# A Strassen-type FFN output product: its seven products chained in PSUM, two of them and the context tokens in plain float32

## The chip, the cores and the metric

The kernel runs on one core of a Trainium2 chip. The metric is the device time of one execution in microseconds. A profiled execution has a span, from its first to its last instruction, and granted clocks of TensorE; all rows below come from one such execution of the kernel before.

## What is computed

Two layers of a trunk over 1024 latent tokens and 256 context tokens of width 1024. Each layer mixes tokens (convolution, retention, attention) and ends in a SwiGLU FFN with a norm behind it. The change touches the FFN's second product alone:

```python
def swiglu(h, w1, w2):
    u, gt = jnp.split(h @ w1, 2, axis=-1)
    return (jax.nn.silu(gt) * u) @ w2          # w2: 2816 x 1024

x = x + g2 * rmsnorm(swiglu(latent), post2_g)    # both layers
xc = xc + cg2 * rmsnorm(swiglu(context), post2_g)    # first layer only
```

Everything is float32 in and out.

## The kernel before

A product that has to be exact in float32 is made of three matmuls in a rounded format (`F32R`): an operand x is split by ScalarE into a rounded high part h (`split`, cast at L85) and by VectorE or GpSimd into the rest l = x - h (L80, `tt`), and TensorE adds h*h, l*h and h*l into one PSUM bank (`mms`, L105). A plain `F32` operand can also go into a matmul as it is; the modulation vectors (`mod_mm`, L209) and the attention's weighting (L1037) do that.

The gated values of the FFN lie in DRAM (`gd`, 22 blocks of 128 rows, 1280 tokens in layer 0, 1024 in layer 1). The second product multiplies them with `ffn_out`, 22 row blocks of 128 x 1024. The first 18 blocks (`NB`) go through a seven-product scheme of the Strassen kind on 2 x 2 blocks of 512: tokens in two halves, row blocks in pairs, output columns in two halves. `groups` makes one group of two row blocks (one pair per product) and four of four (two pairs). `operands` loads a group's values A and weights B (`raw`, `gr`, `wr` tiles by SP's DMA queue), makes sums and differences of quarter blocks in place (`each`), splits them (`two`, `both`) into `gh`, `gl`, `wh`, `wl` with four buffers each, and yields the products in the order 1, 2, 7, 6, 5, 3, 4. Three products are prepared ahead of TensorE.

For each product TensorE works through four token tiles, each into its own bank of PSUM (tag `po`: eight banks in the last layer, six in layer 0), and the bank is added into one of 28 accumulators in SBUF (`evacuate`: VectorE, the group 0 a copy by ScalarE at L1525). There is one accumulator set for each of the seven products; after the last group the `fuse` steps, and in the last layer two more steps in the tail, combine them into the four output blocks. Accumulators appear in the trace as `p`.

In layer 0 the 256 context tokens ride along without the scheme: their values (`gc`) are split, and products 1, 0, 2 and 3 of each group each begin with the context's matmuls on the same split weights (tag `cx`, two banks).

The last four row blocks of all tokens are done in the tail, tile by tile, with the norm, the residual (`postnorm`), the next layer's norm (`rms_tile`) and transposes (`next_pair`) behind each tile. The tail follows the loop directly; in layer 0 it runs over eight latent and two context tiles. Instructions are put into each engine's queue by a scheduler that starts from program order and may move one ahead when an earlier one is not ready.

Of the kernel before, what the change touches and what calls it, by code (L numbers as in the profile page):

```python
# [43 lines left out]
def body(tc, I, out):  # L44
# [465 lines left out]
    for l in range(L):  # L510
# [929 lines left out]
        psum(**({"po": 8} if last else {"po": 6, "cx": 2}))  # L1440
# [5 lines left out]
        hs = ExitStack()  # L1446
        acc = {n: [yp.tile([128, 512], F32, name=f"p{n}{l}{t}") for t in range(4)] for n in (2, 3, 4, 5)}
        ya = {t: (acc[2][t], acc[3][t]) for t in range(4)}
        ya.update({t + 4: (acc[4][t], acc[5][t]) for t in range(4)})
        if not last:  # L1450
            ya.update({t: [yp.tile([128, 512], F32, name=f"pc{l}{t}{hf}") for hf in range(2)] for t in CTX})
        hp = (fs if last else hs).enter_context(pool(f"fx{l}"))
        acc.update({n: [hp.tile([128, 512], F32, name=f"p{n}{l}{t}") for t in range(4)] for n in (1, 6, 7)})
# [3 lines left out]
        gc = gs.enter_context(pool(f"fc{l}", side="right"))  # L1457
        wr = gs.enter_context(pool(f"fw{l}", 4, side="right"))
        V, P, lo, hi = nc.vector, nc.gpsimd, slice(0, 512), slice(512, 1024)

        def operands(js, k):
# [10 lines left out]
            if not last:  # L1472
                C = gc.tile([128, 4, 256], F32, name="gc", tag="gc")
                nc.sync.dma_start(out=C[:, :2 * n], in_=gd[js[0]:js[0] + 2 * n, :, T:NTOK].rearrange("j p n -> p j n"))
# [7 lines left out]
            def two(p, q, nm, x, eng):  # L1482
                h, l = p.tile([128, 1024], F32R, name=nm[0], tag=nm[0]), q.tile([128, 1024], F32R, name=nm[1], tag=nm[1])
                for i in range(n):
                    c = slice(i * 512, i * 512 + 512)
                    split(h[:, c], l[:, c], x[i], None, eng)
                return h, l

            def both(a, b, ea, eb):
                return two(gp, gp, ("gh", "gl"), a, ea), two(whp, wlp, ("wh", "wl"), b, eb)  # L1490

            p1 = both(a11, b11, P, P)
            if not last:
                ch, cl = (gc.tile([128, 4, 256], F32R, name=f"gc{x}", tag=f"gc{x}") for x in "hl")
                split(ch[:, :2 * n], cl[:, :2 * n], C[:, :2 * n], None, P)
                ctx.append((ch, cl))
            yield 1, p1
            yield 2, both(a12, b21, P, P)
            if not last:
                yield 0, (None, two(whp, wlp, ("wh", "wl"), b12, V))  # L1500
# [17 lines left out]
        ops = ((k, n, len(js) // 2, o) for k, js in enumerate(groups) for n, o in operands(js, k))  # L1518
        ctx, cps = [], {}

        def evacuate(k, a, ps, op):
            if k:
                tt(a, a, ps, op)
            else:
                nc.scalar.copy(a, ps)  # L1525

        ahead = [next(ops) for _ in range(3)]
        while ahead:
            k, n, m, (a_, (bh, bl)) = ahead.pop(0)
            if not last and n in (0, 1, 2, 3):  # L1530
                ch, cl = ctx[k]
                for t in CTX:
                    if n in (0, 1):
                        cps[t] = bank("cx")
                    for i in range(m):
                        c, d, q = slice((t - 8) * 128, (t - 8) * 128 + 128), slice(i * 512, i * 512 + 512), 2 * i + n // 2
                        mms(cps[t], [(ch[:, q, c], bh[:, d]), (cl[:, q, c], bh[:, d]), (ch[:, q, c], bl[:, d])],
                            n < 2 and i == 0, n > 1 and i == m - 1)
                    if n > 1:
                        evacuate(k, ya[t][n - 2], cps[t], add)  # L1540
# [179 lines left out]
```

## Time and profile before

| what | value |
|---|---|
| time, median of 3 runs | 3200.51 us (3197.03 to 3209.38) |
| the profiled execution's own time | 3198.45 us |
| its span | 3196.7 us |
| TensorE busy (PE) | 2936.5 us, 92% of the span |
| VectorE (DVE), ScalarE (ACT), GpSimd (POOL) busy | 2310.3, 1196.4, 1489.7 us |
| mean granted TensorE clock | 0.967 of 2.4 GHz |
| loop of the second product, layer 0 | 1464.8 to 1727.9 us |
| loop of the second product, layer 1 | 2936.9 to 3139.2 us |

Matmuls are pipelined: a row's duration is longer than the distance to the next start, so work on TensorE is counted here by starts. A row of the window view gives, for a stretch, the busy time of each engine and how many instructions it ran, then the granted clock, the DMA engines' busy share and what they moved. A row of the group view gives the count, the busy time, the mean duration and the idle time of the engine before them with what ended it.

### The profile page before, as it was taken

What the parts mean: (1) busy time and instruction counts of PE and PEld (TensorE: products, weight loads), DVE (VectorE), ACT (ScalarE), POOL (GpSimd) and SP (SyncE); (2) the same over time, 40 slices, a digit from 0 to 9 for tenths busy, and PEclk for the clock granted to TensorE, in tenths of its full rate; (3) what the DMA queues carried; (4) which work ended last, traced back from release to release, by engine and by line L of the source; (5) the groups of instructions that cost most, each with busy time, mean ns of one, the idle gap of its engine ahead of it and who ended that gap; (6) DMA issues with size and microseconds to landing.
All of it is one profiled execution on the core that took longest, in us unless ns stands there. A gap on an engine that the chain in (4) does not pass through costs nothing. (4 is left out here: it accounts for less than half of the span.)

```text
span 3196.7 us, 39725 instructions
## 1 busy us (share of the span) xinstructions
PE 2936.5 (92%) x13968; PEld 2271.7 (71%) x13968; DVE 2310.3 (72%) x3254; ACT 1196.4 (37%) x2354; POOL 1489.7 (47%) x1187
## 2 busy tenths in 40 slices
PE   7989989889879999999898898989999899999897
PEld 3667865557768888887776676865568678887675
DVE  4388467767897676655888868468856986666998
ACT  4213545553332222225332513545554332224432
POOL 1274535544432232325774365435644343334993
PEclk9989989999989999999999999999999999999998
DMA  7421157657522322213303421157764332224213
GB/s 278 141 67 34 58 178 182 167 129 255 198 81 98 105 91 91 91 65 138 112 20 109 152 66 48 44 184 178 180 181 155 99 113 86 86 81 154 96 66 119
DMA packets 178527, 381.47 MB, mean 119 GB/s; under 512 B 43255, under 2 KB 77687, under 8 KB 178072
## 3 DMA queue, kind: packets, MB, share of 16 engines
q1 hardware_dynamic: 172980, 360.03, 36.8%
q10 hardware_dynamic: 5348, 18.90, 1.4%
q8 instruction: 111, 1.82, 0.2%
q14 instruction: 88, 0.72, 0.1%
HBM read 242.97 MB, written 76.90 MB: 100 GB/s over the span
## 5 line engine op out<-in xcount | busy, mean ns | idle before, releaser
L80 POOL TENSOR_TENSOR wl<-raw,wh 128x512 fp32r<-128x512 f32 (+2 forms) x208 | 387.3, 1874 | 648.3 <-ACT wh L85 648.1
L85 ACT CAST wh<-raw 128x512 fp32r<-128x512 f32 (+2 forms) x305 | 237.6, 796 | 414.9 <-PE pp L105 190.1
L80 DVE TENSOR_TENSOR w<-pp,w 128x512 f32<-128x512 f32 x308 | 207.4, 686 | 186.2 <-PE pp L105 183.9
L994 DVE TENSOR_REDUCE nm<-S 128x1 f32<-128x1280 f32 (+1 forms) x144 | 196.3, 1363 | 89.4 <-PE S L105 87.9
L105 PE MATMUL po<-wh,gh 128*128 128x512 f32 x504 | 203.0, 403 | 35.8 <-DVE p L80 29.3
L999 ACT ACTIVATE P<-S,nm 128x1280 f32<-128x1280 f32 x120 | 159.4, 1329 | 196.6 <-DVE nm L994 196.6
L1026 POOL COPY PT<-T 32x1280 f32<-32x1280 f32 x120 | 150.0, 1250 | 177.3 <-PE mm L1011 116.6
L80 POOL TENSOR_TENSOR rr<-rv,mh 128x1 f32<-128x1 f32 (+2 forms) x130 | 93.1, 717 | 279.6 <-DVE rv L190 277.3
L105 PE MATMUL po<-wh,gl 128*128 128x512 f32 x504 | 200.1, 397 | 0.0
L105 PE MATMUL po<-wl,gh 128*128 128x512 f32 x504 | 199.5, 396 | 0.0
L584 DVE SCALAR_TENSOR_TENSOR cacc<-cy,cw,cacc 128x1295 f32<-128x1295 f32 (+1 forms) x120 | 193.7, 1655 | 0.0
L80 POOL TENSOR_TENSOR gl<-gr,gh 128x512 fp32r<-128x512 f32 x112 | 172.8, 1567 | 27.5 <-ACT gh L85 27.5
L80 POOL TENSOR_TENSOR wl<-sx,wh 128x1024 fp32r<-128x1024 f32 x44 | 109.5, 2488 | 155.9 <-ACT wh L85 155.9
L1091 DVE STREAM_TRANSPOSE T<-P 128x1280 f32<-128x1280 f32 x120 | 180.0, 1500 | 0.0
L1037 PE MATMUL po<-PT,vr 128*64 128x512 f32 x600 | 161.8, 636 | 9.6 <-POOL PT L1026 2.9
L80 DVE TENSOR_TENSOR raw<-raw 128x512 f32<-128x512 f32 (+1 forms) x96 | 127.5, 1336 | 50.5 <-POOL wl L80 47.6
L105 PE MATMUL S<-kh,qh 96*128 96x512 f32 (+1 forms) x384 | 154.3, 402 | 9.9 <-ACT P L999 8.2
L80 DVE TENSOR_TENSOR p<-p,po 128x512 f32<-128x512 f32 x224 | 145.3, 677 | 16.6 <-PE po L105 16.1
L105 PE MATMUL S<-kh,ql 96*128 96x512 f32 (+1 forms) x384 | 143.0, 372 | 9.2 <-POOL ql L80 9.2
L80 DVE TENSOR_TENSOR wl<-raw,wh 128x512 fp32r<-128x512 f32 (+1 forms) x105 | 125.3, 1202 | 28.0 <-ACT wh L85 27.9
L105 PEld LDWEIGHTS po<-wh,gh 128*128 128x128 f32 x504 | 96.9, 192 | 67.5 <-DVE p L80 34.9
L105 PE MATMUL S<-kl,qh 96*128 96x512 f32 (+1 forms) x384 | 142.6, 371 | 0.0
(437 smaller groups left out, 8703.7 us busy)
## 6 DMA issues: line engine op xcount, KB each, us to landing
PT<-T SPq DMA_DIRECT2D x360, 160.0 KB
raw<-in_mod_w SPq DMA_DIRECT2D x96, 512.0 KB
raw<-in_ffn_in SPq DMA_DIRECT2D x88, 512.0 KB
gd<-w SPq DMA_DIRECT2D x88, 256.0 KB
gr<-gd SPq DMA_DIRECT2D x32, 512.0 KB
xs<-x ACTq DMA_DIRECT2D x28, 512.0 KB
raw<-in_ffn_out SPq DMA_DIRECT2D x28, 512.0 KB
x<-xs SPq DMA_DIRECT2D x26, 512.0 KB
```

The lines of the kernel that those rows point to most:

```text
L80: (eng or nc.vector).tensor_tensor(out=out, in0=a, in1=b, op=op)
L85: nc.scalar.copy(h, t)
L105: nc.tensor.matmul(ps, lhsT=a, rhs=b, start=start and i == 0, stop=stop and i == len(xs) - 1)
L584: nc.vector.scalar_tensor_tensor(out=acc[:, ct, :], in0=y0[:, ct, j:j + AW], scalar=w, in1=acc[:, ct, :], op0=mult, op1=add)
L994: nc.vector.reduce_max(out=u.nm, in_=ps[:, :nk], axis=AX.X, negate=True)
L999: nc.scalar.activation(out=P, in_=u.ps, func=AF.Exp, bias=u.nm, accum_out=u.sm)
L1026: nc.gpsimd.tensor_copy(o, i)
L1037: nc.tensor.matmul(u.po[64 * (j % 2):64 * (j % 2) + 64], lhsT=u.hd.v[:, j, :], rhs=src[:, :, j * 32:j * 32 + 32], start=j < 2, stop=j > 7)
L1091: nc.vector.transpose(out=T1[:, :, u.a // 128].rearrange("p c (k i) -> p k c i", i=32), in_=u.P.rearrange("p (k c i) -> p k c i", c=4, i=32))
```

## The change

The loop over seven products is rebuilt. PSUM is divided in two sets of four banks, `pa` and `pb`, one bank per token tile in each. Product 1 opens a bank of `pa`, and products 6, 5 and 3 of the same group go on adding to that bank; product 2 opens a bank of `pb`, product 7 opens a new one, product 4 goes on in it. After each product VectorE adds the bank as it then stands into one of four output accumulators (`acc` "11", "12", "21", "22"), so a bank is read between two products that add to it. The 12 accumulators of products 1, 6, 7 and all combining steps go. Products 1 and 2 take their operands unsplit, as plain float32, one matmul for each triple of before. Products 5 and 4 have their weights' low parts made by GpSimd, not VectorE.

In layer 0 the context tokens are done ahead of the loop: all 22 row blocks in plain float32 into the four `pb` banks, with their values loaded in two pieces and the weights loaded a first time for this alone. Their norms come after the first group, and their tiles leave the tail; their transposes are queued at the tail's first tick.

```diff
-        psum(**({"po": 8} if last else {"po": 6, "cx": 2}))
+        psum(pa=4, pb=4)
...
+        if not last:
+            gc = gs.enter_context(pool(f"fc{l}", side="right"))
+            C = gc.tile([128, NJ, 256], F32, name="gc")
+            for j in range(0, NJ, 11):
+                nc.sync.dma_start(out=C[:, j:j + 11], in_=gd[j:j + 11, :, T:NTOK].rearrange("j p n -> p j n"))
+            cps = {(t, hf): bank("pb") for t in CTX for hf in range(2)}
+            for j in range(NJ):
+                b = wr.tile([128, 1024], F32, name="wr", tag="wr")
+                nc.sync.dma_start(out=b, in_=I["ffn_out"][l, j])
+                for (t, hf), ps in cps.items():
+                    nc.tensor.matmul(ps, lhsT=C[:, j, (t - 8) * 128:(t - 8) * 128 + 128], rhs=b[:, hf * 512:hf * 512 + 512],
+                                     start=j == 0, stop=j == NJ - 1)
+            for (t, hf), ps in cps.items():
+                nc.scalar.copy(ya[t][hf], ps)
...
-            p1 = both(a11, b11, P, P)
...
-            yield 1, p1
-            yield 2, both(a12, b21, P, P)
-            if not last:
-                yield 0, (None, two(whp, wlp, ("wh", "wl"), b12, V))
+            yield 1, list(zip(a11, b11))
+            yield 2, list(zip(a12, b21))
...
-            yield 5, both(a11, b12, P, V)
+            yield 5, both(a11, b12, P, P)
...
-            each(b21, b11, b21, sub, V)
-            yield 4, both(a22, b21, P, V)
+            each(b21, b21, b11, sub, V)
+            yield 4, both(a22, b21, P, P)
...
+        CHAIN = {1: ("pa", True, "11"), 2: ("pb", True, "11"), 7: ("pb", True, "22"), 6: ("pa", False, "21"),
+                 5: ("pa", False, "22"), 3: ("pa", False, "12"), 4: ("pb", False, "21")}
...
+            b, first, o = CHAIN[n]
+            for t in range(4):
+                if first:
+                    held[b, t] = bank(b)
+                ps, a = held[b, t], acc[o][t]
+                c = slice(t * 128, t * 128 + 128)
+                for i, (x, y) in enumerate(terms):
+                    nc.tensor.matmul(ps, lhsT=x[:, c], rhs=y, start=first and i == 0, stop=i == len(terms) - 1,
+                                     skip_group_check=not first)
+                if (o, t) in begun:
+                    tt(a, a, ps, add)
+                else:
+                    begun.add((o, t))
+                    nc.scalar.copy(a, ps)
...
+            if not last and k == 0 and n == 4:
+                ce = gs.enter_context(pool(f"fe2{l}", side="right"))
+                G = load_G(ce, l, 1, 1)
                 for t in CTX:
...
+                    x = load_x(ce, t)
+                    postnorm(x, ya[t], ya[t], G, new_x(l, 1, t))
+                    rms_tile(x, ya[t], ya[t])
...
-            if end:
-                if n == 2:
-                    fuse(2, 2, 1, add, P)
-                elif n == 6:
-                    fuse(6, 6, 1, add)
-                    fuse(7, 7, 6, add)
-                elif n == 5:
-                    fuse(6, 6, 5, add)
-                    if not last:
-                        fuse(5, 5, 7, add)
...
-        for t in tiles:
+        if not last:
+            tk.later(1, next_pair, 8)
+        for t in LAT:
...
-            if last and t < 4:
-                tt(acc[4][t], acc[7][t], acc[4][t], sub)
-                tt(acc[5][t], acc[5][t], acc[7][t], add)
```

## Rows read from the trace of the kernel before

**Rows 1.** The page's first part: busy us, share of the span, instructions.
```profile
PE 2936.5 (92%) x13968; PEld 2271.7 (71%) x13968; DVE 2310.3 (72%) x3254; ACT 1196.4 (37%) x2354; POOL 1489.7 (47%) x1187
```

**Rows 2.** Busy time by stretch: layer 0's loop and its opening, layer 1's.
```profile
core 0: us, PE busy (x) PEld busy (x) DVE busy (x) ACT busy (x) POOL busy (x), PEclk, DMA share, GB/s
1464.80:1727.90 263.10, 230.90 (x973) 186.01 (x973) 215.36 (x252) 97.67 (x172) 187.00 (x122) 0.95 0.28 95
1464.80:1484.00 19.20, 13.61 (x47) 10.01 (x47) 8.55 (x11) 9.52 (x18) 9.35 (x8) 0.82 0.82 307
...
2936.90:3139.20 202.30, 182.02 (x756) 143.32 (x756) 187.65 (x209) 84.48 (x153) 180.48 (x112) 0.97 0.31 110
3085.00:3121.50 36.50, 36.50 (x162) 30.03 (x160) 35.94 (x41) 10.58 (x19) 34.87 (x22) 1.00 0.17 58
3139.00:3160.00 21.00, 19.49 (x72) 15.15 (x73) 18.48 (x31) 3.83 (x10) 4.34 (x4) 0.83 0.18 64
```

**Rows 3.** The same by tile: instructions on `po`, then on `cx`; no POOL column.
```profile
1464.80:1727.90 263.10, 181.59 (x756) 144.58 (x756) 73.30 (x112) 15.14 (x28) 0.95 0.28 95
...
1464.80:1727.90 263.10, 55.29 (x216) 41.41 (x216) 10.57 (x16) 2.23 (x4) 0.95 0.28 95
```

**Rows 4.** Timeline of TensorE in layer 0's loop: start us, duration us, instruction.
```profile
1579.31 0.39 PE L105 MATMUL po<-wh,gh 128*128 128x512 f32 x1
1579.53 0.39 PE L105 MATMUL po<-wh,gl 128*128 128x512 f32 x1
1579.76 0.39 PE L105 MATMUL po<-wl,gh 128*128 128x512 f32 x1
```

**Rows 5.** Plain float32 matmuls of `mod_mm`: durations min/median/max in ns; one timeline row.
```profile
L209 PE MATMUL rx<-raw,cs x96: 591/592/592, 54.9 to 132.6; 128*2 128x512 f32 x96
L209 PE MATMUL mm<-raw,cs x64: 591/592/1061, 6.1 to 35.7; 128*2 128x512 f32 x64
...
54.91 1.03 PE L209 MATMUL rx<-raw,cs 128*2 128x512 f32 x4
```

**Rows 6.** TensorE's waits in the loops, layer 0 then 1: us, times, longest.
```profile
PE po L105 <- DVE p L80: 18.2, 4, 11.5
PE cx L105 <- DVE pc L80: 6.8, 3, 2.3
...
PE po L105 <- DVE p L80: 11.0, 7, 4.2
```

**Rows 7.** VectorE's groups in layer 1's loop: count, busy us, mean ns, idle before.
```profile
L80 DVE TENSOR_TENSOR p<-p,po 128x512 f32<-128x512 f32 x106 | 68.3, 675 | 0.0
L80 DVE TENSOR_TENSOR wl<-raw,wh 128x512 fp32r<-128x512 f32 x20 | 25.7, 1286 | 4.0 <-ACT wh L85 4.0
L80 DVE TENSOR_TENSOR raw<-raw 128x512 f32<-128x512 f32 x17 | 22.4, 1316 | 2.1 <-POOL wl L80 1.8 <-DMA raw<-in_ffn_out 0.4
L80 DVE TENSOR_TENSOR p<-p,p 128x512 f32<-128x512 f32 x16 | 20.9, 1361 | 0.0
...
L80 DVE TENSOR_TENSOR gr<-gr 128x512 f32<-128x512 f32 x16 | 20.0, 1257 | 1.4 <-DMA gr<-gd 1.4
```

**Rows 8.** GpSimd's largest group in the same stretch.
```profile
L80 POOL TENSOR_TENSOR gl<-gr,gh 128x512 fp32r<-128x512 f32 x56 | 88.9, 1616 | 1.7 <-ACT gh L85 1.7
```

**Rows 9.** Timeline: TensorE at the loops' ends, with its idle time before.
```profile
1722.17 0.79 PE L105 MATMUL po<-wh,gh 128*128 128x512 f32 x1 [11.54 <-DVE p L80]
...
3139.23 0.77 PE L105 MATMUL mm<-wh,hh 128*128 128x512 f32 x1 [7.71 <-DVE p L80]
```

**Rows 10.** Timeline of SP's DMA queue at the opening of layer 0's loop.
```profile
1468.33 0.41 SPq L1474 DMA_DIRECT2D gc<-gd  x1
...
1469.57 0.32 SPq L1331 DMA_DIRECT2D gd<-w  x1
```

**Rows 11.** VectorE's groups in layer 0's tail: two of the context's norm.
```profile
L445 DVE SCALAR_TENSOR_TENSOR x<-pc,rr,x 128x512 f32<-128x512 f32 x4 | 5.0, 1272 | 0.4 <-POOL rr L80 0.4
L80 DVE TENSOR_TENSOR pc<-pc,G 128x512 f32<-128x512 f32 x4 | 4.9, 1235 | 0.2 <-DMA G<-gd 0.2
```

More of the change, by code (lines that the diff above doesn't have):

```diff
@@ L1486, in two @@
                     split(h[:, c], l[:, c], x[i], None, eng)
[L1487 removed]
+                return [(h[:, i * 512:i * 512 + 512], l[:, i * 512:i * 512 + 512]) for i in range(n)]
             def both(a, b, ea, eb):
[L1490 to L1500 removed]
+                x, y = two(gp, gp, ("gh", "gl"), a, ea), two(whp, wlp, ("wh", "wl"), b, eb)
+                return [z for (ah, al), (bh, bl) in zip(x, y) for z in ((ah, bh), (al, bh), (ah, bl))]
+            yield 1, list(zip(a11, b11))
+            yield 2, list(zip(a12, b21))
             each(a21, a11, a21, sub, V)
@@ L1517, in body @@
             groups.insert(0, list(range(NB % 4)))
[L1518 to L1525, printed above, removed]
+        ops = ((k, n, o) for k, js in enumerate(groups) for n, o in operands(js, k))
+        CHAIN = {1: ("pa", True, "11"), 2: ("pb", True, "11"), 7: ("pb", True, "22"), 6: ("pa", False, "21"),
+                 5: ("pa", False, "22"), 3: ("pa", False, "12"), 4: ("pb", False, "21")}
@@ L1527, in body @@
+        begun, held = set(), {}
         ahead = [next(ops) for _ in range(3)]
         while ahead:
-            k, n, m, (a_, (bh, bl)) = ahead.pop(0)
-            if not last and n in (0, 1, 2, 3):
-                ch, cl = ctx[k]
-                for t in CTX:
[L1533 to L1540, printed above, removed]
@@ L1541, in body @@
-            ahead.extend([x for x in [next(ops, None)] if x])
-            if not n:
-                continue
-            ah, al = a_
-            end = k == len(groups) - 1
-            def fuse(o, x, y, op, eng=None):
-                for t in range(4):
-                    tt(acc[o][t], acc[x][t], acc[y][t], op, eng)
-            if end and n == 3:
-                fuse(3, 3, 6, add, None if last else P)
-                if not last:
-                    fuse(4, 7, 4, sub)
-            for t in range(4):
-                ps = bank("po")
-                for i in range(m):
-                    c, d = slice(i * 512 + t * 128, i * 512 + t * 128 + 128), slice(i * 512, i * 512 + 512)
-                    mms(ps, [(ah[:, c], bh[:, d]), (al[:, c], bh[:, d]), (ah[:, c], bl[:, d])], i == 0, i == m - 1)
-                evacuate(k, acc[n][t], ps, sub if end and n == 4 and not last else add)
@@ L1561, in body @@
-            if end:
-                if n == 2:
-                    fuse(2, 2, 1, add, P)
-                elif n == 6:
-                    fuse(6, 6, 1, add)
-                    fuse(7, 7, 6, add)
-                elif n == 5:
-                    fuse(6, 6, 5, add)
-                    if not last:
-                        fuse(5, 5, 7, add)
+            k, n, terms = ahead.pop(0)
+            if n != 1:
+                ahead.extend([x for x in [next(ops, None)] if x])
+            b, first, o = CHAIN[n]
@@ L1571, in body @@
+            if n == 1:
+                ahead.extend([x for x in [next(ops, None)] if x])
+            if not last and k == 0 and n == 4:
+                ce = gs.enter_context(pool(f"fe2{l}", side="right"))
+                G = load_G(ce, l, 1, 1)
+                for t in CTX:
+                    x = load_x(ce, t)
+                    postnorm(x, ya[t], ya[t], G, new_x(l, 1, t))
+                    rms_tile(x, ya[t], ya[t])
         gs.close()
-        hs.close()
         psum(mm=4, rx=1, ry=1, aux=2)
```

16 lines of the change are left out of this document (5 added, 11 removed).

## Prediction

> **What bounds the kernel now.** I read the page's first part, then the busy times by stage, then who waited for whom inside the two stages that the change rewrites, then the instruction groups of those stages. Over the whole run TensorE is busy 92% of the span [rows 1], but that share is no guide to one stage. The second FFN product takes 263.1 us in layer 0 and 202.3 us in layer 1 [rows 2]. TensorE runs 756 + 216 = 972 matmuls in the first and 756 in the second [rows 3]; in a full stream one starts every 0.227 us [rows 4], so their bare work is 220.6 and 171.6 us. The rest, 42.5 and 30.7 us, is waiting. In layer 1 VectorE is busy 187.7 of 202.3 us and GpSimd 180.5 [rows 2], and nearly all that TensorE waits for is VectorE's adds into the partial sums [rows 6]: there TensorE, VectorE and GpSimd stand close together and VectorE ends last. In layer 0 TensorE stands higher (220.6 of 263.1, VectorE 215.4). Both stages end in a queue of combining adds on VectorE: TensorE stands 11.5 us before its last product of layer 0 and 7.7 us before the tail of layer 1 [rows 9].
>
> **Plain float32 on TensorE.** Products 1 and 2 lose their splits; each triple of split matmuls (3 x 0.227 = 0.68 us) becomes one plain float32 matmul. Its price is the term that decides. The modulation product is such a matmul with 512 columns: the code issues 80 of them (5 calls of 16) and the trace has 64 + 96 = 160 records [rows 5], so one matmul is two records. A record lasts 592 ns against 0.39 us for a split one [rows 4, 5], that is 0.20 us more on a start-to-start of 0.227: 0.43 us per record. Four records that share the array by pairs take 1.03 us, so the second pair starts 1.03 - 0.59 = 0.44 us after the first [rows 5]. So 0.86 us per matmul, with bounds 0.81 (four times 0.20) and 0.88. It is dearer than the triple it replaces by 0.18 us.
> Per layer: 2 products x 4 tiles x 9 pairs of row blocks = 72 plain matmuls, 61.9 us, in place of 216 x 0.227 = 49.0: +12.9. The other five keep 540 x 0.227 = 122.6. Latent work is 184.5 us per layer.
> Context, layer 0 only: 4 sums x 22 row blocks = 88 plain matmuls, 75.7 us, in place of 216 in the loop and 48 in the tail (59.9): +15.8. In all TensorE gets +41.6 us (232 plain matmuls; the bounds move this by -12 and +5).
>
> **What it takes from VectorE and GpSimd.** Layer 1, VectorE: the splits on it fall from 36 to 18 halves (products 5 and 4 move to GpSimd), -18 x 1.29 = -23; the combining adds go, 16 of them, 20.9 us, between loop and tail; sums by VectorE rise by 12 because only 16 first tiles, not 28, are plain copies by ScalarE, +12 x 0.675 = +8; the 54 in-place steps stay at about 1.3 us [rows 7]. So 124 x 0.675 + 54 x 1.27 + 18 x 1.29 = 175 us, down from 188. GpSimd: 108 half operations become 90, x 1.6 us [rows 8] = 145, down from 180. With 184.5 us TensorE is then last, by 10 us. A full group of four row blocks is 42.5 us of TensorE against 38 of VectorE and 32 of GpSimd.
> What two engines do to each other, on the rows: VectorE's adds with one operand in PSUM take 0.675 us, those with both in SBUF 1.26 to 1.36 while GpSimd works [rows 7]. By the Trainium skill, SBUF — State Buffer, section "Who interferes with whom", a VectorE instruction with two SBUF inputs contends with a GpSimd instruction that reads SBUF, and one with a single SBUF input does not; the rows agree. By that rule GpSimd's smaller share would shorten VectorE's 72 steps too, which adds nothing to the sum where TensorE is last but speaks for the faster case below.
>
> **Waits that go, and what is late next.** The end of layer 0's loop (11.5 us) and of layer 1's (7.7 us) go with the combining adds: after the last product come four adds of 0.675 us, and the tail's first banks are free earlier. I keep 2 us at each end. The tail of layer 1 begins after 7.7 us without a matmul, and its first 21 us were granted 0.83 [rows 2], in part the lower of the two levels (1.2 GHz); without that idle time I expect 2.4 GHz there, 21 x 0.17 = 3.6, taken as -3 us.
> New waits: product 1 and 2 read the raw operands, so the in-place steps on them (VectorE's on b11 and b21, GpSimd's on a11 and a12) wait for TensorE. Queued behind them on VectorE are the next split and the sums of product 2, on GpSimd the splits for product 5. From the end of product 1 there are two products (7 + 5.5 us) until the first such operand is needed, and its chain is two steps, a cast and a split, some 8 us: cost nothing in full groups; with one pair per product (the first group) 1 to 2 us.
> The sums are read between products of a chain: product 5's tile may start only when VectorE has added product 6's from the same bank, three tiles (3 x 6 x 0.227 = 4.1 us) later. Four adds take 2.7 us. Waits of this kind were 11.0 us in layer 1 with eight banks [rows 6]; I take 1 us per group, 4 per layer, with bounds 0 and the rival's.
>
> **The context ahead.** Its first matmul needs the gate values of half the row blocks and a weight tile; 2.9 MB of values (1 KB pieces) and 0.5 MB stand on SP's queue before the first weight tile lands. Layer 0's stage could issue such loads at 1468.3 us, behind the last stores of the gate values [rows 10]; the stage's first 19.2 us moved 307 GB/s at a share of 0.82 [rows 2], 374 GB/s when all engines work. So 3.4 / 0.374 = 9.1 us: not before 1477.4, that is 12.5 us after the stage begins. Products 1 and 2 of the first group need only loads that were issued long before, 8 plain matmuls, 6.9 us, and can run first. The stage of before lost 8.5 us in the same place (47 matmuls, 10.7 us, in the first 19.2 us [rows 2]). I take 8 us, with bounds 3 and 17 (nothing runs first, gate buffers still held until the store at 1469.6 has landed).
> Then 22 weight tiles of 0.52 MB, one per 3.44 us of TensorE, 153 GB/s where 374 were seen: hidden, with four buffers; SP waits there for TensorE's release, and the loads of group 1 stand behind it, due 20 us later. If that cover fails, each wait shows whole.
> The context's norms leave the tail and come behind the first group: VectorE gets 2 x (2 x 1.24 + 2 x 1.27 + 2 x 0.6 + small ones 0.7) = 14 us [rows 11], GpSimd four short powers, ScalarE eight passes, SP one gain and two x loads. Group 1 has 42.5 - 38 = 4.5 us to spare on VectorE, the later ones too; I take 5 us of delay (0 to 14). The tail loses 48 matmuls (11 us) and two tiles' VectorE work: -13.
>
> **Sum.** Layer 0's stage: 184.5 + 75.7 + 8 + 5 + 4 + 2 = 279, against 263: +16; tail -13; together +3. Layer 1's: 184.5 + 2 (first group) + 4 + 2 = 193, against 202: -9; tail -3; together -12. Net -9 on the profiled execution of 3198.45 us (span 3196.7 and 1.75 around it), which is 2 us under the median of 3200.51: 3190 us. 41.6 us of dearer TensorE work is paid by some 50 us of waits.
>
> **Rivals.** *TensorE alone counts.* The first group's products cover the loads, the norms vanish in VectorE's spare time, chains never wait: layer 0 260 + 3 + 2, layer 1 184.5 + 2 + 2, tails -16: 263 + 202 become 265 + 188.5 less 16, net -28, at the low end of the price down to -38: about 3170. For it: from 3085 to 3121.5 us before ran 162 matmuls in 36.5 us, without a wait, though VectorE was busy 35.9 of them [rows 2]; against: no stage of before ran without waits.
> *The bank chain waits (slower).* Edges 2 to 7, 6 to 5 and 5 to 3 stay in one set of four banks, 3 x 10 groups. The cover falls from seven tiles (9.5 us) in layer 1 and five (6.8 us) in layer 0 to 4.1 us. VectorE's queue has up to two in-place steps and a split (some 6 us) ahead of a product's sums; from a lag of 4.1 us on, each edge costs. At 1 us per edge beyond my 8 us it is +22 or more, and a lag of 5.4 us gives +30: 3212 to 3222, say 3220. For it: TensorE's waits on VectorE's sums [rows 6]; against: VectorE has 10% to spare. By the Trainium skill, Perfetto Trace Analysis, section "Matmuls", independent groups should rotate through different banks so that the evacuation of one overlaps the next; the chain gives some of this up, and that rule is this rival.
> *The context's opening is not covered*: 17 us, and norms at 14: 9 + 9 = +18 on the forecast, 3208.
> *It does not do what it says*: a plain matmul with one record, 0.43 us, would give 100 us back; the count of 160 records for 80 matmuls [rows 5] speaks against it.
>
> **Chances.** Forecast 0.50 (its own range 3181 to 3200, a fifth of it below 3184), TensorE alone 0.24, bank chain 0.17, opening 0.08, other price 0.01. What a measurement can tell from no change is about 0.5%, 16 us: below 3184.5 or above 3216.5. Faster: 0.24 + 0.10 + 0.01 = 0.35; same: 0.40 + 0.08 = 0.48; slower 0.17. Range 3170 to 3216: it leaves out half of the chain's chance and the far end of the fast case.
>
> **What would show it.** Two records per plain matmul, 0.42 to 0.44 us apart, 464 of them; no wait of TensorE over 3 us behind the last product of either layer; layer 1's stage 190 to 197 us with VectorE below 95%; layer 0's context stretch 76 us without waits from its second weight tile on. I am wrong if TensorE's waits on VectorE's sums exceed 10 us in a layer, or if the loads open the stage with over 12 us of idle TensorE.

## The result and the profile after

The changed kernel takes 3223.4 us (median of 7 runs, 3212.1 to 3229.8) where the kernel before took 3203.9 beside it (7 runs, 3197.0 to 3211.3): 1.0062 of the time before, 95% interval 1.0045 to 1.0079. Slower by 0.6%; the forecast was 3190 us, faster by 0.3%, and its range ended at 3216.

The busy times by stretch (columns as in [rows 2]): layer 0's loop, layer 1's, layer 1's tail, the context's stretch.

```profile
1470.00:1762.50 292.50, 268.84 (x862) 161.69 (x861) 175.93 (x220) 69.29 (x128) 146.49 (x97) 0.99 0.40 135
2966.70:3174.80 208.10, 191.72 (x686) 126.90 (x685) 166.09 (x196) 61.75 (x109) 148.38 (x93) 1.00 0.29 104
3174.80:3228.00 53.20, 45.60 (x193) 35.70 (x192) 39.27 (x65) 15.32 (x39) 16.38 (x15) 0.95 0.45 159
1484.80:1560.40 75.60, 75.59 (x176) 33.55 (x177) 3.46 (x5) 2.33 (x6) 0.00 (x0) 1.00 0.66 226
```

VectorE and GpSimd did get lighter in layer 1's loop (187.7 to 166 us, 180.5 to 148 [rows 2]), TensorE's granted clock there is 1.00, and still the stage isn't shorter. The spans of single profiles are no measure of this change: the parts that it doesn't touch differ by up to 10 us from profile to profile (up to the loop of layer 0 between 1461 and 1471 us in the kernels below, between the stages 1068 to 1078). So stages are compared. Each is read from the starts of matmuls on the timeline: a loop from the start of the last matmul of the product ahead of it to the first of its tail, a tail to the next layer's first own work or to the end. (By this reading layer 1's loop before begins at 2933.75 us; [rows 2] begins at its own first matmul, 2936.9, so its 202.3 us are 205.5 here.) Each stage is read from one profile of each kernel: layer 1's loop repeats within 0.5 us where its code is the same in the changed kernel, e2 and e9, and within 1.8 us in e14 and e15; for layer 0's loop there is no such repeat. All kernels of this study (the names are explained below; e11 leaves out a part of the arithmetic, so its time is a measure of the banks and no alternative):

| kernel | loop 0 | tail 0 | loop 1 | tail 1 | median | ratio to before, 95% |
|---|---|---|---|---|---|---|
| before | 263.3 | 137.5 | 205.5 | 57.4 | | |
| after | 292.6 | 126.0 | 208.1 | 53.2 | 3223.4 | 1.0045 to 1.0079 |
| e1_fresh | 285.8 | 126.0 | 204.8 | 53.5 | 3210.4 | 1.0003 to 1.0028 |
| e2_norm_tail | 289.6 | 125.4 | 208.1 | 53.2 | 3220.0 | 1.0028 to 1.0053 |
| e3_split | 295.5 | 124.5 | 204.5 | 53.2 | 3218.5 | 1.0024 to 1.0050 |
| e4_swap | 311.2 | 126.0 | 223.1 | 53.2 | 3255.5 | 1.0132 to 1.0167 |
| e6_fresh_late | 285.5 | 124.5 | 205.5 | 53.2 | 3210.2 | 0.9999 to 1.0027 |
| e7_late | 296.0 | 126.0 | 208.0 | 53.2 | 3220.6 | 1.0038 to 1.0083 |
| e9_ctx_split | 289.5 | 124.2 | 208.6 | 53.2 | 3213.4 | 1.0022 to 1.0056 |
| e11_free_banks | 286.7 | 124.6 | 189.0 | 53.5 | 3194.4 | 0.9958 to 0.9991 |
| e13_alt | 305.2 | 125.1 | 213.2 | 54.2 | 3238.9 | 1.0095 to 1.0129 |
| e14_alt_fresh | 295.9 | 124.1 | 205.4 | 53.2 | 3218.5 | 1.0031 to 1.0059 |
| e15_alt_fresh_ctx_end | 262.4 | 126.9 | 203.6 | 53.2 | 3191.7 | 0.9945 to 0.9975 |
| e17_no_edges | 253.3 | 127.1 | 193.0 | 53.2 | 3172.8 | 0.9869 to 0.9905 |

Before to after: loop 0 +29.3, tail 0 -11.5, loop 1 +2.6, tail 1 -4.2, together +16.2 of the 19.5 us between the medians. The loops are what has to be explained. Their waits, TensorE's alone (us, times, longest; to be read beside [rows 6]), layer 0 and then layer 1:

```profile
PE pb L1541 <- ACT wh L85: 9.0, 4, 7.6
PE pb L1541 <- DVE p L80: 5.2, 3, 1.7
PE pa L1541 <- ACT wh L85: 3.1, 1, 3.1
PE pa L1541 <- DVE p L80: 2.5, 5, 0.6
PE pa L1541 <- ACT gh L85: 1.8, 1, 1.8
PE pb L1470 <- DMA gc<-gd: 1.6, 1, 1.6
...
PE pb L1541 <- DVE p L80: 8.3, 6, 1.7
PE pa L1541 <- DVE p L80: 5.4, 4, 1.9
PE pb L1541 <- ACT wh L85: 1.4, 3, 0.5
...
```

The 11.5 and 7.7 us at the ends of the loops [rows 9] are gone, as forecast. In their place stand many small ones, and the larger part sits at one place that comes back in every group: product 7, which opens `pb` anew behind product 2 (the rows with `pb`); the chain 6, 5, 3 in `pa` has most of the others. Here is that place in the last group, on TensorE's timeline (start us, duration us, instruction, idle time before with its releaser). One row of product 2, and the start of each tile of product 7:

```profile
3137.40 1.88 PE L1541 MATMUL pb<-raw,gr 128*128 128x512 f32 x4
...
3144.89 0.47 PE L1541 MATMUL pb<-wh,gh 128*128 128x512 f32 x1 [0.46 <-ACT wh L85]
...
3146.48 0.50 PE L1541 MATMUL pb<-wh,gh 128*128 128x512 f32 x1
...
3148.18 0.50 PE L1541 MATMUL pb<-wh,gh 128*128 128x512 f32 x1
...
3151.57 0.50 PE L1541 MATMUL pb<-wh,gh 128*128 128x512 f32 x1 [1.74 <-DVE p L80]
```

And VectorE's timeline of the same stretch, first four of the sums while products 4 and 1 run, then on from behind product 1's last sum:

```profile
3126.65 0.69 DVE L80 TENSOR_TENSOR p<-p,pb 128x512 f32<-128x512 f32 x1 [0.68 <-PE pb L1541]
3128.01 0.69 DVE L80 TENSOR_TENSOR p<-p,pb 128x512 f32<-128x512 f32 x1 [0.67 <-PE pb L1541]
...
3132.45 0.69 DVE L80 TENSOR_TENSOR p<-p,pa 128x512 f32<-128x512 f32 x1 [1.03 <-PE pa L1541]
3134.16 0.69 DVE L80 TENSOR_TENSOR p<-p,pa 128x512 f32<-128x512 f32 x1 [1.03 <-PE pa L1541]
...
3139.62 1.16 DVE L80 TENSOR_TENSOR raw<-raw 128x512 f32<-128x512 f32 x1
3140.71 1.76 DVE L80 TENSOR_TENSOR wl<-raw,wh 128x512 fp32r<-128x512 f32 x1
3142.39 1.75 DVE L80 TENSOR_TENSOR raw<-raw 128x512 f32<-128x512 f32 x1
3144.07 0.68 DVE L80 TENSOR_TENSOR p<-p,pb 128x512 f32<-128x512 f32 x1
3144.66 1.17 DVE L80 TENSOR_TENSOR wl<-raw,wh 128x512 fp32r<-128x512 f32 x1
3145.75 0.67 DVE L80 TENSOR_TENSOR p<-p,pb 128x512 f32<-128x512 f32 x1
3146.35 1.18 DVE L80 TENSOR_TENSOR wl<-raw,wh 128x512 fp32r<-128x512 f32 x1
3147.45 0.67 DVE L80 TENSOR_TENSOR p<-p,pb 128x512 f32<-128x512 f32 x1
3148.05 1.18 DVE L80 TENSOR_TENSOR wl<-raw,wh 128x512 fp32r<-128x512 f32 x1
3149.15 1.76 DVE L80 TENSOR_TENSOR raw<-raw 128x512 f32<-128x512 f32 x1
3150.84 0.68 DVE L80 TENSOR_TENSOR p<-p,pb 128x512 f32<-128x512 f32 x1
```

The two lists fit tooth by tooth. The sums of product 2 end at 3144.75, 3146.42, 3148.12 and 3151.52; the tiles of product 7, which take over those four banks, start 0.14, 0.06, 0.06 and 0.05 us later. (The first is put down to ScalarE's `wh`, the others show as matmuls further apart or as a wait on `p`: the pairs of times say more than the releaser's name. By the order of the steps, product 7's own last low part was ready at 3119.65 on GpSimd's timeline, and the cast that ends just ahead of its first tile is a later product's.) Product 2's first matmul starts at 3137.40, a tile of it takes 1.72 us, and a record lasts 0.59, so its banks are complete at 3139.3, 3141.0, 3142.7 and 3144.4: the sums end 5.4 to 5.5 us behind that, the last one 7.1. Without waiting, product 7 would have begun each tile 5.0 to 3.9 us behind. And VectorE isn't short of time as a whole: through products 4 and 1 it waits 0.67 to 1.03 us ahead of each sum but product 1's last. Its preparation comes in bunches; in this one each sum stands behind one step that takes 1.1 to 1.7 us from start to start, the last behind two. From the end of the first sum to that of the fourth lie 6.8 us, and a split product takes 5.45.

What holds the preparation back until then is told by GpSimd's row in the same stretch: it stands 14.2 us until product 1 has read the operand that it overwrites.

```profile
3136.78 3.45 POOL L80 TENSOR_TENSOR gr<-gr 128x512 f32<-128x512 f32 x2 [14.18 <-PE pa L1541]
```

So there were two candidates that the trace alone doesn't part: the *operands* that the plain products hold, which bunch the work, and the *banks*, whose short cover (the tiles of work between two uses of a bank) turns a late sum into a wait. From the last record of product 2 to the first of product 6 lie 9.2 us in seven of the eight full groups, where 5.9 (0.43 and 5.45) are bare work, and 15.5 in layer 0's first. In that one the sum of product 2's first tile ends 12.7 us behind its bank. And there the wait costs more than it lasts: the granted clock is 0.50 from 1594.6 to 1598.2 us, behind 8.2 us from one matmul's start to the next, and the matmuls stand 0.43 us apart in place of 0.227.

### The profile page after: what moved, and what is told of

The parts are those of the page before. It is cut to its first block, busy times and chain, and to the rows that moved or that the text cites. A ratio compares the mean times of both kernels' runs of the same rounds, so it can differ in the third digit from the quotient of the medians.

```text
span 3228.0 us, 38979 instructions
## 1 busy us (share of the span) xinstructions
PE 2986.1 (93%) x13736; PEld 2235.0 (69%) x13736; DVE 2222.1 (69%) x3169; ACT 1135.9 (35%) x2242; POOL 1410.3 (44%) x1132
## 5 line engine op out<-in xcount | busy, mean ns | idle before, releaser
L85 ACT CAST wh<-raw 128x512 fp32r<-128x512 f32 (+2 forms) x280 | 221.7, 811 | 301.5 <-PE pp L105 180.7
L1326 ACT ACTIVATE w<-w 128x512 f32<-128x512 f32 x88 | 55.6, 631 | 239.8 <-DVE w L80 239.8
L263 DVE SCALAR_TENSOR_TENSOR macc<-raw,cs,macc 128x512 f32<-128x512 f32 x140 | 132.8, 971 | 3.9 <-DMA raw<-in_mod_w 2.7
L105 PEld LDWEIGHTS S<-kh,qh 96*128 96x128 f32 x384 | 76.9, 200 | 83.3 <-issue 34.5
L80 POOL TENSOR_TENSOR gl<-gr,gh 128x512 fp32r<-128x512 f32 x80 | 121.8, 1541 | 2.2 <-ACT gh L85 1.8
L80 DVE TENSOR_TENSOR p<-p,pa 128x512 f32<-128x512 f32 x136 | 89.9, 681 | 43.4 <-PE pa L1541 43.1
L85 ACT CAST gh<-gr 128x512 fp32r<-128x512 f32 x80 | 48.2, 620 | 198.9 <-POOL gr L80 163.6
L105 PE MATMUL mm<-wl,m_h 128*128 128x512 f32 x288 | 114.4, 397 | 3.9 <-POOL wl L80 3.3
```

The source lines that it names most:

```text
L80: (eng or nc.vector).tensor_tensor(out=out, in0=a, in1=b, op=op)
L85: nc.scalar.copy(h, t)
L105: nc.tensor.matmul(ps, lhsT=a, rhs=b, start=start and i == 0, stop=stop and i == len(xs) - 1)
L263: nc.vector.scalar_tensor_tensor(out=accs[w], in0=r[:, i], scalar=cs[:, k + i, w:w + 1], in1=accs[w], op0=mult, op1=add)
L1326: nc.scalar.activation(out=th, in_=u, func=AF.Tanh, scale=0.5)
```

## The experiments

**In-place sums in tiles of their own (e1_fresh).** The theory here was the operands; the rival, the banks.

```diff
-            each(b11, b12, b11, add, V)
-            yield 6, both(a21, b11, P, V)
-            each(a11, a21, a11, add, P)
...
+            each(fb, b12, b11, add, V)
+            yield 6, both(a21, fb, P, V)
+            each(fa, a21, a11, add, P)
...
-            if n != 1:
-                ahead.extend([x for x in [next(ops, None)] if x])
+            ahead.extend([x for x in [next(ops, None)] if x])
```

> The changed kernel, but the sums that replaced b11, a11, a12 and b21 in place are written elsewhere (two new tiles, and a21), so that no VectorE or GpSimd step waits for TensorE to have read the plain operands of products 1 and 2; the preparation is queued three products ahead for product 1 too. Theory W (the in-place waits): in the changed kernel GpSimd stands 14 us and VectorE some 10 us per group until product 1 is done, then their steps pile up in front of product 2's sums, and product 7, which reuses product 2's banks, loses 3.3 us per group (four groups per layer). Without the waits layer 1's loop goes from 207.9 us to 190 to 197, layer 0's from 292.4 to 277 to 285; the whole 3190 to 3205 where the changed kernel takes 3223. Theory B (banks alone): product 7 still waits for product 2's sums, four banks being too few; loops within 3 us of the changed kernel, 3218 to 3228. Theory P (the dearer plain matmuls are the whole loss): the same, 3218 to 3228.

Loops 285.8 and 204.8: the operands give 6.8 and 3.3 us, far less than the theory asked for, and more than the rival's 3. TensorE's waits in layer 1 moved more than they went:

```profile
PE pa L1543 <- DVE p L80: 7.8, 8, 2.0
PE pb L1543 <- DVE p L80: 4.5, 2, 4.2
```

Product 7 no longer waits in the last three groups; the first full group and the chain 6, 5, 3 wait instead, again for sums.

**The context's norms back in the tail (e2_norm_tail).** The block of `postnorm` and `rms_tile` for `CTX` goes from behind the first group to the end of layer 0's tail, and the context's transposes with it.

> The changed kernel, but the context's norms stand at the end of layer 0's tail, where they were before the change, not behind the first group. Theory N (the norms in the loop cost more there than they save in the tail): the 8.2 us wait of TensorE before product 7 of the second group falls to the 1 us that the later groups show, and the loop shortens by 8 to 12 us; the tail grows by 3 to 6 us, since the context's matmuls stay out of it; the whole 3215 to 3221. Rival (the wait is the first full group's, due to loads and the pile of steps, not the norms'): the loop stays within 3 us, the tail grows by 6 to 10, the whole 3226 to 3235. Layer 1 within 2 us in both.

Loop 0 -3.0, tail 0 -0.6: by one profile of each, the norms cost 3.6 us where they are; neither case came out as written down. In the first full group of layer 0 the way from product 2's last record to product 7's first falls from 8.24 to 3.40 us, but the matmuls behind it then stand 0.358 us apart in the mean, in place of 0.308: the granted clock, 0.50 again, stays low longer here (1588.7 to 1594.8 us). The rest of the place's loss isn't the norms'.

**Products 1 and 2 split again (e3_split).**

```diff
-            yield 1, list(zip(a11, b11))
-            yield 2, list(zip(a12, b21))
+            yield 1, both(a11, b11, P, P)
+            yield 2, both(a12, b21, P, P)
```

> The changed kernel, but products 1 and 2 of the latent tokens are split again into three matmuls each (GpSimd makes all their low parts); the chain in four and four banks, the four sums and the context ahead stay. Theory P (plain price): TensorE gets back 12.9 us of work per layer, and the loops shorten by 10 to 13 us each: layer 1 195 to 198 us, the whole 3198 to 3204. Theory W: GpSimd has 126 half operations of 1.6 us, 202 us, for 171.6 us of TensorE work and ends last: layer 1 200 to 212 us, the whole 3215 to 3235; the wait before product 7 goes, since nothing waits for plain operands. Theory B: the wait of product 7 for product 2's banks stays at 3 us per group.

TensorE's bare work falls by 12.9 us per layer; the loops come to 295.5 and 204.5, +2.9 and -3.6, so the plain products' price does not come back as time. With 171.6 us of bare work, layer 1's loop loses 33 us. But this run alone doesn't part the price from what the splits load on GpSimd: it is busy 189.2 of the 204.5 us, near the 202 that the expectation had for it.

**Product 2 ahead of product 1 (e4_swap).** The two `yield` lines change places, so that product 7 stands behind another set's product, and the operands of product 1 are held one product longer.

> The changed kernel, but product 2 comes before product 1, so that product 1 (6.9 us) lies between product 2 and product 7, which takes product 2's banks again; the in-place steps on product 1's operands start one product later. Theory B (banks): the 3.3 us per group at product 7 go, layer 1's loop 194 to 199 us, layer 0's 280 to 286, the whole 3198 to 3208. Theory W (in-place waits): the pile of steps comes 6.9 us later, with one product of 5.5 us as its cover, so that product 6 or 5 waits 3 to 8 us per group instead: layer 1's loop 207 to 225, the whole 3223 to 3255.

Loops 311.2 and 223.1, much slower. Product 7 is free; in layer 1's full groups product 6, which needs the operands of product 1 summed, waits 1.8 us for its split, and products 5 and 3 behind it wait 1.0 to 2.9 us at a time for sums. It bears out that a held operand can cost, when its use follows closely. It does not settle which of the two costs in the changed kernel, since both were moved.

**The order of preparation and sums (e6_fresh_late, e7_late).** Each preparation is written behind the running product's sums: e7 with the in-place sums, e6 with tiles of their own.

```diff
             k, n, terms = ahead.pop(0)
-            if n != 1:
-                ahead.extend([x for x in [next(ops, None)] if x])
...
                     nc.scalar.copy(a, ps)
-            if n == 1:
-                ahead.extend([x for x in [next(ops, None)] if x])
+            ahead.extend([x for x in [next(ops, None)] if x])
```

> The in-place sums go to tiles of their own, as in the run with fresh tiles, and besides the preparation of a coming product is written behind the running product's four sums, not ahead of them. Two causes together (operands held by the plain products, and a queue on VectorE that puts preparation ahead of sums while a bank is waited for): loop of layer 1 188 to 196 us, of layer 0 272 to 283, the whole 3190 to 3207. If only the banks' short cover matters, whatever the queue's order: layer 1 stays at 203 to 208, the whole 3208 to 3216.

> Only the order: the in-place sums stay in place, the preparation of a coming product is written behind the running product's sums. If the order on VectorE's queue is the main cause: layer 1 195 to 201 us, the whole 3205 to 3214. If the operands held by the plain products are the main cause, the order alone changes little: layer 1 204 to 210, the whole 3216 to 3228.

Loop 1 205.5 and 208.0, as without the new order (204.8 and 208.1); loop 0 285.5 and 296.0 (285.8 and 292.6). In the program's order the sums now come first, and nothing is gained by it; the theory that put the loss on the written order falls.

**The context split (e9_ctx_split).** Each triple of split matmuls for one plain matmul in the context's stretch:

```diff
-                    nc.tensor.matmul(ps, lhsT=C[:, j, (t - 8) * 128:(t - 8) * 128 + 128], rhs=b[:, hf * 512:hf * 512 + 512],
-                                     start=j == 0, stop=j == NJ - 1)
...
+                    mms(ps, [(ch[:, o:o + 128], bh[:, d]), (cl[:, o:o + 128], bh[:, d]), (ch[:, o:o + 128], bl[:, d])],
+                        j == 0, j == NJ - 1)
```

> The context tokens ahead of the loop are computed with split operands, three matmuls of 0.227 us for one plain matmul of 0.86; the splits lie on engines that stand idle in that stretch. 88 x (0.86 - 0.68) = 15.8 us of TensorE less. If the plain price is what layer 0 loses there: the stretch 60 to 63 us for 75.6, layer 0's loop 277 to 282, the whole 3206 to 3213. If the splits on VectorE become the bound of the stretch (22 blocks x two halves x 1.3 us = 57 us, beside the cast on ScalarE): stretch 66 to 72 us, the whole 3213 to 3220.

The stretch goes from 75.6 to 64 us, near the fast case. But loop 0 gains 3.1 us only, not the 11 to 16 of that case: the context's first split needs the loads first and then a cast and a rest, and products 6 and 5 of the first group, which run ahead of the context in the changed kernel, come behind it here. TensorE stands at the opening (us, times, longest):

```profile
PE pb L105 <- ACT gh L85: 11.6, 1, 11.6
```

**No product goes on in another's bank (e11_free_banks).** This one parts the two candidates: operands stay in place, and each product takes four fresh banks out of eight in turn. What it leaves out is the carry of a product into the later sums of its group.

```diff
-        psum(pa=4, pb=4)
+        psum(po=8)
...
-                if first:
-                    held[b, t] = bank(b)
-                ps, a = held[b, t], acc[o][t]
+                ps, a = bank("po"), acc[o][t]
...
-                    nc.tensor.matmul(ps, lhsT=x[:, c], rhs=y, start=first and i == 0, stop=i == len(terms) - 1,
-                                     skip_group_check=not first)
+                    nc.tensor.matmul(ps, lhsT=x[:, c], rhs=y, start=i == 0, stop=i == len(terms) - 1)
```

> No product goes on in another's bank: each opens a new one out of eight in turn, so a sum has seven tiles of cover, not three. It leaves out the carrying of a product into the later sums of its group; the number of matmuls, sums and preparations stays as it is. If the banks' short cover (4.1 us) is the main cause: layer 1 192 to 199 us, layer 0 280 to 285, the whole 3200 to 3211. If the operands held by the plain products are the main cause, the wait comes from the split ahead of product 7 all the same: layer 1 203 to 208, the whole 3213 to 3224.

Layer 1's loop falls from 208.1 to 189.0 us, more than even the banks' own forecast of 192 to 199, with 184.5 us of bare work. TensorE's waits in it, and VectorE's timeline at the same place of the last group:

```profile
PE po L1539 <- DVE p L80: 1.5, 2, 1.0
PE po L1539 <- DVE w L80: 1.3, 1, 1.3
...
3114.31 0.67 DVE L80 TENSOR_TENSOR p<-p,po 128x512 f32<-128x512 f32 x1
3114.91 1.18 DVE L80 TENSOR_TENSOR wl<-raw,wh 128x512 fp32r<-128x512 f32 x1
3116.01 0.67 DVE L80 TENSOR_TENSOR p<-p,po 128x512 f32<-128x512 f32 x1
...
3117.71 0.68 DVE L80 TENSOR_TENSOR p<-p,po 128x512 f32<-128x512 f32 x1
...
3119.41 1.78 DVE L80 TENSOR_TENSOR raw<-raw 128x512 f32<-128x512 f32 x1
3121.11 0.67 DVE L80 TENSOR_TENSOR p<-p,po 128x512 f32<-128x512 f32 x1
...
3122.82 6.20 DVE L80 TENSOR_TENSOR p<-p,po 128x512 f32<-128x512 f32 x10
```

VectorE's queue is the same, step for step: the same bunch, the same 1.7 us from sum to sum, the same late fourth sum. TensorE runs past it, since its next banks are empty, and VectorE makes up for it afterwards with ten sums in a row. The bunch costs nothing at this place, where the cover is seven tiles. In layer 0 the loop falls by 5.9 us only, but its opening is another: the context begins after 15.1 us without a matmul (products 1, 6 and 5 don't run ahead), where the changed kernel loses 5.7 at the same place, and its stretch takes 2.6 us longer, with a granted clock of 0.50 in its first 3.3 us. The four full groups stand behind all that, the changed kernel's and then e11's:

```profile
1573.10:1762.50 189.40, 171.18 (x609) 114.17 (x608) 153.04 (x188) 50.27 (x89) 133.34 (x87) 0.98 0.24 82
...
1584.20:1754.00 169.80, 166.09 (x609) 113.60 (x608) 144.68 (x182) 49.64 (x87) 127.76 (x84) 1.00 0.25 84
```

They fall by 19.6 us. The first, small group is 1.7 us longer, so the banks are worth some 18 us in layer 0, an estimate.

**The two sets take turns (e13_alt, e14_alt_fresh).** Nothing is left out here: the order 2, 1, 7, 6, 4, 5, 3 puts a product of the other set between any two that share banks, except between 5 and 3. e13 keeps the in-place sums, e14 gives them tiles of their own (as in e1).

```diff
-            yield 1, list(zip(a11, b11))
             yield 2, list(zip(a12, b21))
+            yield 1, list(zip(a11, b11))
...
+            each(b21, b21, b11, sub, V)
+            yield 4, both(a22, b21, P, P)
             each(a11, a21, a11, add, P)
             each(b12, b22, b11, sub, V)
             yield 5, both(a11, b12, P, P)
             each(a12, a12, a21, sub, P)
             yield 3, both(a12, b22, P, V)
-            each(b21, b21, b11, sub, V)
-            yield 4, both(a22, b21, P, P)
...
```

> Order 2, 1, 7, 6, 4, 5, 3: the two sets of banks take turns, so that between two products that use one bank lies a whole product of the other set, and the cover of a sum is seven tiles (9.5 us), but for 5 to 3. Operands stay in place; nothing is left out. The run with product 2 first and 6, 5, 3 behind one another had 311 and 223 us. If the banks' cover is the main cause: layer 1 194 to 206 us, layer 0 288 to 298, the whole 3207 to 3230. If the operands that product 1 holds until late (the sum for product 6 waits for it) are the main cause, turns don't help: layer 1 215 to 224, the whole 3240 to 3256.

> The same turns of the banks and the in-place sums in tiles of their own, so that no operand is held by products 1 and 2. If cover and operands are all that the loops lose: layer 1 187 to 194 us (bare work 184.5), layer 0 278 to 286, the whole 3188 to 3203, no slower than the kernel before. If the order in VectorE's queue costs whatever the banks and operands are: layer 1 200 to 206, the whole 3206 to 3216.

TensorE's waits in layer 1's loop, e13's two largest and e14's only one:

```profile
PE pa L1541 <- DVE p L80: 10.1, 3, 5.1
PE pa L1541 <- DVE wl L80: 9.3, 5, 2.0
...
PE pa L1543 <- DVE p L80: 12.9, 7, 3.8
```

e13 against e4: turns take 9.9 us off layer 1's loop (223.1 to 213.2) and 6 off layer 0's, and leave the 9.3 us of product 6 waiting for the held operand's split; the times lie between the two cases that were written down. e14 takes that wait away too (205.4) and misses its forecast of 187 to 194 all the same; it lies in its rival's range, VectorE's queue at 200 to 206, and only e17 parts the two. Of the 12.9 us of waits that are left, 10.5 stand ahead of tiles of product 3, at the one edge without turns, the rest in product 6 of the first full group. The waits of three kinds of edges have gathered at one, and their sum is no less than e1's 12.3. Besides, the granted clock of this loop is 0.97, where the changed kernel's was 1.00: it is 0.50 from 3027 to 3031 us, behind the longest wait of 3.8 us. That the edge would take nothing over was wrong.

**The context behind the loop (e15_alt_fresh_ctx_end).** e14, and the context's 22 row blocks follow the last group, split, their values loaded while group 1 runs, their norms at the end of the tail.

```diff
+            if not last and k == 1 and n == 2:
+                for j in range(0, NJ, 11):
+                    nc.sync.dma_start(out=C[:, j:j + 11], in_=gd[j:j + 11, :, T:NTOK].rearrange("j p n -> p j n"))
...
+        if not last:
+            cps = {(t, hf): bank("pb") for t in CTX for hf in range(2)}
+            for j in range(NJ):
...
```

> Turns and own tiles as above; besides the context tokens come behind the last group with split operands (60 us of TensorE for 76), their values loaded while group 1 runs, and their norms at the end of the tail. Nothing is left out. If the opening (6 to 15 us), the norms in the loop (4) and the plain price (15) are what layer 0 loses beyond that: its loop 250 to 262 us, its tail 125 to 133, layer 1 187 to 194, the whole 3160 to 3185, faster than the kernel before. If what is saved at the opening comes back as a wait at the end of the loop (splits of the context, the tail's first banks): loop 265 to 280, the whole 3183 to 3200.

Loop 0 falls from 295.9 to 262.4 us with the tail at 126.9: opening, norms and plain price, 33.5 us in all, come off, which leaves the loop just beyond the far end of the 250 to 262 expected; 2.8 us come back in the tail, none at the loop's end. The context's 264 matmuls run at 0.227 us without a gap. Layer 1 keeps its edge (203.6, not the 187 to 194 written down), and with it the whole misses its 3160 to 3185: 3191.7 us, 0.25 to 0.55% under the kernel before.

**No edge left (e17_no_edges).** e15, with product 3 in a bank of its own and the sets' roles changed from group to group; product 5's bank is added into two outputs, and the low parts of product 3's weights go to GpSimd.

```diff
-    5: ("pa", False, "22"), 3: ("pa", False, "12"), 4: ("pb", False, "21")}
+    5: ("pa", False, "22"), 3: ("pb", True, "12"), 4: ("pb", False, "21")}
...
+            if k % 2:
+                b = "pb" if b == "pa" else "pa"
...
+                for q in ((o, "12") if n == 5 else (o,)):
...
-            yield 3, both(a21, b22, P, V)
+            yield 3, both(a21, b22, P, P)
```

> As the run before it with the context behind the loop, but product 3 opens a bank of its own and the sets change their roles from group to group, so that a whole product of the other set lies between any two products that use one bank. Price: product 5's bank is added twice, 4 sums of 0.675 us more per group (13 us of VectorE in a layer), and the low parts of product 3's weights go from VectorE to GpSimd (9 halves). Nothing is left out. If the one remaining edge (5 to 3) is what layer 1's loop still loses (203.6 against 184.5 bare): layer 1 187 to 193 us, layer 0's loop 252 to 257, the whole 3165 to 3182. If VectorE's and GpSimd's amount of work is the bound whatever the edges: layer 1 198 to 206, the whole 3186 to 3200.

By stretch: layer 1's loop, then three full groups of each layer; then TensorE's waits in layer 1's loop.

```profile
2929.70:3122.70 193.00, 186.86 (x686) 128.27 (x685) 160.32 (x207) 61.20 (x109) 152.63 (x102) 1.00 0.31 112
2999.80:3122.70 122.90, 122.90 (x458) 85.84 (x457) 94.40 (x130) 30.71 (x53) 91.05 (x63) 1.00 0.19 61
1541.20:1664.10 122.90, 122.90 (x458) 85.92 (x457) 99.21 (x133) 32.52 (x54) 89.87 (x61) 1.00 0.26 86
...
PE pb L1537 <- DVE p L80: 5.8, 4, 1.7
```

Three full groups in a row without a wait in each layer: 122.9 us for three, 41.0 each, which is their bare work (16 plain matmuls x 0.86 and 120 split ones x 0.227). VectorE isn't lighter for it (160.3 us in layer 1's loop, 159.6 in e14's), and GpSimd has more (152.6 and 144.6), so the amount of work was not the bound. What is left in layer 1 are 5.8 us of waits, 5.2 of them in product 6 of the first full group, where the banks' roles change while VectorE still has the first group's pile. 3172.8 us: 0.9887 of the time before (0.9869 to 0.9905), and 51 us under the changed kernel, with the same plain products 1 and 2 and more sums than it had. Both loops and the whole came out inside what was written for the edge as the cause, layer 1's at its upper end (187 to 193).

## Why the prediction was wrong, point by point

**Right.** The price of plain float32: its matmuls in the loop and in the context's stretch are two records each, of 592 ns (by form: duration of the shortest, median and longest in ns, first and last start; the weight load of the context between them),

```profile
L1541 PE MATMUL pa<-wr,gr x32: 590/592/593, 2992.6 to 3091.9; 128*128 128x512 f32 x32
L1470 PEld LDWEIGHTS pb<-wr,gc x176: 186/190/191, 1484.8 to 1559.6; 128*128 128x128 f32 x176
L1470 PE MATMUL pb<-wr,gc x176: 592/592/667, 1484.8 to 1560.0; 128*128 128x512 f32 x176
```

0.429 us apart where nothing waits, as [rows 5] gave it; the context's stretch took 75.6 us for 75.7, its weight stream was hidden. The opening lost 5.7 us for a forecast of 8, but partly by luck: product 2 could not run first as written, since the context holds the four `pb` banks, and products 6 and 5 ran in its place. The end waits went, to 0.23 us from matmul to matmul between loop and tail. Tail 0 gave 11.5 for 13, tail 1 4.2 for 3 with its clock at 0.95. The norms in the loop cost 3.6 for 5. VectorE's and GpSimd's work came to 166 and 148 us for 175 and 145.

**The step that failed** is the price of the chain's edges: "I take 1 us per group, 4 per layer". Free banks take 19.1 us off layer 1's loop and, by the estimate above, some 18 off layer 0's: 37 in place of 8. That covers the whole miss, 25 us: the stages came out at +16.2 where the sum had -9. And the rest of the sum holds in layer 1: without the 4 us its forecast was 189, which is what e11 took. The prediction's own sign of being wrong, waits on VectorE's sums of over 10 us in a layer, came true there: 8.3 and 5.4 us.

**Where the sizing went wrong.** The rival of the bank chain had the mechanism, the three edges, the cover and, with an assumed lag of 5.4 us, 30 us and 3220; the trace shows lags of 5.4 to 7.1 in the last group. That the assumed lag fits so closely is luck: the loss isn't spread over all edges, 3.3 us stand at product 7 in a full group of layer 1 and most of the rest at product 3. The rival was given 17% because VectorE "has 10% to spare". That share is a mean over a loop. It was also too high for a full group: "42.5 us of TensorE" should be 41.0 by the prediction's own terms (184.5 us x 2 pairs of 9), which leaves 3 us beside VectorE's 38 and not 4.5. An edge asks how late one sum is in the worst stretch of a group, and the rows of the kernel before could have told it: a sum behind one in-place step or split takes 0.675 + 1.3 us [rows 7], four of them 7.9, and a product 5.45. The rule quoted beside that rival is that independent groups should rotate through different banks (the Trainium skill, Perfetto Trace Analysis, section "Matmuls"). e11 agrees with it: with rotating banks the same sums, as late at the place shown, cost TensorE 1.5 us in layer 1's loop.

**Operands in place**, said to "cost nothing in full groups", hold for the changed order in so far as e11, with operands in place and its banks free, has no wait for them. They do bunch VectorE's work, which the step left out, and that costs 3.3 us in layer 1 and 6.8 in layer 0 with the chain as it stands (e1). Where product 6 stands closer behind product 1 (e13 against e14) they cost 7.8 and 9.3 us.

**Still open** is why the scheduler bunches the preparation where it does: with the sums written first (e7) the bunch stays at its place, and with freed operands (e1, e14) product 7 of layer 1 is free in three or all of the four full groups, but the waits come back at other edges.

## What to carry to other kernels

When accumulators move from SBUF into PSUM and products chain in one bank, count for each edge the cover in tiles, and set against it the worst lag of one sum, read from the timeline of the evacuating engine, and not that engine's mean share. Here an engine that was busy 80% of a loop made short edges wait because its work came in bunches, and taking one edge away moved the wait to the next short one. With a whole product of the other bank set between any two products that use one bank (e17), three full groups of each layer ran without a wait, with more sums than before.

## What was not expected of the hardware

A plain float32 matmul shows the same records with 128 columns of weights as with the two of the modulation product: two of 592 ns, 0.429 us from start to start, here with a weight load of 190 ns for each beside it. So 0.86 us for a 128 x 128 by 128 x 512 product in plain float32, against 0.68 for the three split matmuls: what it saves here is the splits of other engines, not TensorE's time. And a stretch that streams all its weights and runs nothing but such matmuls (226 GB/s at a DMA share of 0.66) kept TensorE at 75.59 busy of 75.60 us, at a granted clock of 1.00. Where TensorE had stood waiting the granted clock did fall: to 0.50 behind the 8.2 us in layer 0's first full group, and behind 3.8 us in e14's layer 1.
